# A two-layer encoder on one core: in every fourth weight step, the low part of the weights by an accumulating DMA

## The chip, the core and the metric

The kernel runs on one core of a Trainium2 chip. The metric is the device time of one execution in microseconds (us), the median of the runs; lower is better. The engines are called as the profile calls them: PE (TensorE, matrix products), PEld (its weight loads), DVE (VectorE), ACT (ScalarE), POOL (GpSimd) and SP (SyncE, which here only issues DMAs). SPq stands for SP's instruction queue. All loads of weights and inputs are issued by SP.

## What is computed

x has 256 tokens of 2048 columns, all in float32. Two layers follow each other; each one normalizes, projects, mixes, projects back, normalizes and adds:

```python
h = rmsnorm(x, norm_pre[0])                       # layer 0: gated linear attention
q, k, v, g, glr = split(h @ gla_w_in)             # 2048 x (1024 + 1024 + 2048 + 2048 + 16)
y = attention_by_chunks(q, k, v, glr) * silu(g)
x = x + rmsnorm(y @ gla_w_out, norm_post[0])      # 2048 x 2048

h = rmsnorm(x, norm_pre[1])                       # layer 1: spatial gating
u, v, g = split(h @ sgu_w_in, 3)                  # 2048 x 6144
y = gelu(u) * spatial(layernorm(gelu(v))) * silu(g)
x = x + rmsnorm(y @ sgu_w_out, norm_post[1])      # 2048 x 2048
```

The four big projections carry nearly all of the work. Their weights are read from memory once.

## The kernel before, in words

**Three products for one.** PE multiplies in float32r, which keeps fewer bits than float32. So each operand is kept as two float32r parts, high and low: the high part is the rounded value, the low part what the rounding left over. A product is the sum of three: high by high, low activations by high weights, high activations by low weights (lines 178, 179, 180).

**Groups and steps.** The columns of the weights are taken in 33 groups of up to 512 columns, in this order: two groups q (steps 0 to 15), three groups k of 352, 344 and 344 columns (16 to 39; the first of them is put together from two pieces of the weights), four groups v (40 to 71), four g (72 to 103), four of layer 0's output projection (104 to 135); then layer 1's four groups vg (136 to 167), four u (168 to 199), four sg (200 to 231) and four of its output projection (232 to 263). A group is 8 steps, and a step is two K tiles of 128 rows: one load of 128 x 1024 float32 (512 KB; 344 KB in the narrow groups). Both tiles of 128 tokens (t = 0 and t = 1) use a step's weights, so a step has 2 tokens x 2 K tiles x 3 = 12 products.

**What is done for a step.** `load` (line 91) takes a tile `raw` out of a ring of RAWS = 4 and issues the load on SP (line 98). `split` (line 105) takes tiles `whi` and `wlo` out of rings of SPLITS = 6; ACT copies `raw` to `whi` with rounding (line 110), and then DVE writes `wlo` = `raw` - `whi` (line 111). In a few steps (`pool_lo`, line 134: 0, 2, 4, 6, and 1, 3 and 5 steps behind the start of layer 1, that is 137, 139, 141) POOL does the subtraction in place of DVE.

**Order.** The program is written out by hand, and every engine takes its instructions in that order. `run` (line 188) issues the products of a step for one tile of tokens (`part`), lets each live generator take a stage (`advance`: what follows a group's products, for example the activation, the norms, the transposes), and then calls `fetch` for the steps up to AHEAD = 4 beyond the current one. So behind the products of step i for t = 0 stand the load and the split of step i + 4. At the end of a group the activation of its result for t = 0 stands on ACT just ahead of the split of the next group's step 3. Because step i + 4 stands behind the products of t = 0 alone, this split can begin only when PE is in the middle of the group's last step.

**What a tile waits for.** The load of step i + 4 waits until the split of step i has been done with its `raw` tile; the ring of four makes steps 3, 7, 11, ... share one of the four. ACT's copy for step i waits for its load and for PE's last product with the `whi` of step i - 6. SP's queue is in order too, so a load that waits holds up the loads behind it.

**POOL's other work.** POOL raises the norms to the power -0.5 (line 224), prepares the products with the gains around layer 0's output (lines 605 and 640), and scales and shifts `vg` in the u groups (line 703).

Of the kernel before, what the change touches and what calls it, by code (L numbers as in the profile page):

```python
# [9 lines left out]
F32R = mybir.dt.float32r  # L10
BF16 = mybir.dt.bfloat16
AF = mybir.ActivationFunctionType
ALU = mybir.AluOpType
PSUM = bass.MemoryType.PSUM

P = 128
# [6 lines left out]
KC = 2  # L23
LAG = 5
# [5 lines left out]
SLOTS = 24  # L30
RAWS = 4
SPLITS = 6


@with_exitstack
def trunk(
# [18 lines left out]
    nc = tc.nc  # L55
# [9 lines left out]
    of = out[0]  # L65
# [6 lines left out]
    wraw = ctx.enter_context(tc.tile_pool(name="wraw", bufs=RAWS))  # L72
    wsp = ctx.enter_context(tc.tile_pool(name="wsp", bufs=SPLITS))
    gains = ctx.enter_context(tc.tile_pool(name="gains", bufs=3))
# [12 lines left out]
    def w512(name, dtype=F32):  # L87
        return work.tile([P, 512], dtype, name=name, tag="w512")

# [1 line left out]
    def load(parts, c, fine):  # L91
        w = sum(n for _, _, n in parts)
        raw = wraw.tile([P, KC, w], F32, name="raw", tag="raw")
        at = 0
        for src, c0, n in parts:
            rows = src[c * KC * P : (c + 1) * KC * P, c0 : c0 + n].rearrange("(a p) n -> p a n", p=P)
            for ks in pieces(fine):
                nc.sync.dma_start(raw[:, ks, at : at + n], rows[:, ks, :])
            at += n
        return raw  # L100

    def pieces(fine):
        return [slice(k, k + 1) for k in range(KC)] if fine else [slice(0, KC)]

    def split(raw, eng, fine):
        shape = [P, KC, raw.shape[2]]
        hi = wsp.tile(shape, F32R, name="whi", tag="whi")
        lo = wsp.tile(shape, F32R, name="wlo", tag="wlo")
        for ks in pieces(fine):
            nc.scalar.copy(hi[:, ks], raw[:, ks])  # L110
            eng.tensor_tensor(lo[:, ks], raw[:, ks], hi[:, ks].bitcast(F32), op=ALU.subtract)  # L111
        return hi, lo

    NS = KT // KC

    class Stream:
        """Projections, column group by column group, in steps of KC K tiles; both tiles of
        tokens use a step's weights. What follows a group's products is a generator, whose
        stages come one by one between the parts that follow; a stage may ask for more parts
        before the next. Around a boundary (a group whose operand is the end of all groups  # L120
        before it) the tiles of tokens take turns of LAG steps, so that each one's products
        cover what the other waits for."""

        def __init__(self, groups, boundaries, mid):
            self.mid = mid
# [19 lines left out]
        def fetch(self, i):  # L145
            if i < len(self.steps) and i not in self.split:
                self.load(i)
                eng = nc.gpsimd if i in self.pool_lo else nc.vector
                self.split[i] = split(self.raw[i], eng, i == 0)

        def start(self, gen):
            if gen is not None:
# [35 lines left out]
        def run(self):  # L188
            freed, at = 0, 0
            for i, t in self.order:  # L190
# [4 lines left out]
                at = max(at, i)  # L195
                for j in range(at + 1, min(at + (AHEAD if at >= NS else 2), freed + SPLITS - 1) + 1):
                    self.fetch(j)
# [1 line left out]
                self.advance()  # L199

    def split_T(dst, t, c, tp):
        """Four transposed blocks, from PSUM into the two parts of a product's operand."""
        ah, al = dst
        sl = slice(t * P, (t + 1) * P)
        nc.scalar.copy(ah[c][:, :, sl], tp)  # L205
        nc.vector.tensor_tensor(al[c][:, :, sl], tp, ah[c][:, :, sl].bitcast(F32), op=ALU.subtract)  # L206
# [7 lines left out]
    def new_T(name):  # L214
        return (
            [slot(S4, F32R, f"{name}h{c}") for c in range(4)],
            [slot(S4, F32R, f"{name}l{c}") for c in range(4)],
        )
# [18 lines left out]
        return rstd(s1, D, name)  # L237

    def bcast(vecs, cs):
        """Column groups of vectors, on every partition."""  # L240
        g = gains.tile([P, 2, 512], F32, name="gb", tag="gb")
        for i, (v, c) in enumerate(zip(vecs, cs)):
            nc.sync.dma_start(
                g[:, i, :], v[c * 512 : (c + 1) * 512].unsqueeze(0).to_broadcast([P, 512])
            )
        return g

# [1 line left out]
    xs = [const.tile([P, D], F32, name=f"x{t}", tag=f"x{t}") for t in range(NT)]  # L249
    vec = const.tile([16, P], F32, name="vec")  # L250
    nc.scalar.dma_start(vec, norm_pre[0].rearrange("(a p) -> a p", p=P))
# [6 lines left out]
    make_identity(nc, ident)  # L258
    mhalf = const.tile([P, 1], F32, name="mhalf")
    nc.gpsimd.memset(mhalf, -0.5)  # L260
    # suffix sums within a chunk: U[t', t] = 1/tau where t' > t and both lie in one chunk;
    # the last two columns give the chunks' sums
    U = const.tile([P, P + 2], F32, name="U")
    nc.gpsimd.memset(U, 0.0)
    for c in range(2):
# [8 lines left out]
    gpre0 = const.tile([P, KT], F32, name="gpre0")  # L274
    bsp = const.tile([P, GROUPS], F32, name="bsp")

# [1 line left out]
    hT = new_T("hT")  # L278

    def make_hT(t, c):  # L280
        tp = transpose4(xs[t][:, c * 512 : (c + 1) * 512])
        tmp = w512("ttmp").rearrange("p (a b) -> p a b", b=P)
        gain = gpre0[:, c * 4 : c * 4 + 4].unsqueeze(2).to_broadcast([P, 4, P])
        nc.vector.tensor_tensor(tmp, tp, gain, op=ALU.mult)
        split_T(hT, t, c, tmp)
# [3 lines left out]
    groups = []  # L289

    q, k, la, ek, kd, k2, qT = ([None] * 2 for _ in range(7))
# [14 lines left out]
    for i in range(2):  # L306
        groups.append(dict(parts=[(W, q0 + i * 512, 512)], lhs=lambda: hT, done=q_done(i)))

    # the gate's weights and bias, each part at its own partitions, against the parts of the
    # low-rank activations: one pass gives all four products  # L310
    wg = [None]

    def pre_gate():
# [179 lines left out]
    for i, (c0, n) in enumerate(kcols):  # L493
        parts = [(W, k0 + c0, n)] + ([(W, l0, RANK)] if i == 0 else [])
        groups.append(dict(parts=parts, lhs=lambda: hT, done=k_done(i)))

    on = [None] * HEADS
# [30 lines left out]
    def pre_gain(key, vecs, cs):  # L528
        def f():
            st[key] = bcast(vecs, cs)  # L530
        return f
# [13 lines left out]
    def g_done(h):  # L545
        def f(t, ps):
            if t == 0:
                new_T4("ogT", h, "ogT")
            sg = w512("sg")
            nc.scalar.activation(sg, ps, AF.Silu, scale=r0[t])  # L550
            nc.vector.tensor_tensor(sg, on[h][:, t, :], sg, op=ALU.mult)
            yield 4
            split_T(st["ogT"], t, h, transpose4(sg))
        return f
# [1 line left out]
    for h in range(HEADS):  # L556
        groups.append(dict(parts=[(W, g0 + h * DV, DV)], lhs=lambda: hT, done=g_done(h)))

# [1 line left out]
    def out_groups(key, w_out, gain, name, end, extra=None):  # L560
        yg = [None] * 4
        ss = [small(f"{name}ss{t}", 4) for t in range(NT)]

        def done(c):
            def f(t, ps):
                if t == 0:
                    yg[c] = slot([P, NT, 512], F32, f"{name}g{c}")
                sumsq(ps, ss[t][:, c : c + 1])

                def scale():  # L570
                    if extra is not None:
                        extra(t, c, ps)
                    nc.vector.tensor_tensor(yg[c][:, t, :], ps, st[name][:, c % 2, :], op=ALU.mult)

                if c < 3:
                    scale()
                else:
                    s1 = small(f"{name}s{t}")
                    nc.vector.reduce_sum(s1, ss[t], axis=mybir.AxisListType.X)
                    yield from end(t, yg, rstd(s1, D, f"{name}r{t}"), scale)  # L580
            return f

        gs = [dict(parts=[(w_out, c * 512, 512)], lhs=lambda: st[key], done=done(c)) for c in range(4)]
        for c in (0, 2):
            gs[c]["pre"] = pre_gain(name, [gain] * 2, [c, c + 1])
        return gs
# [6 lines left out]

    r1 = [None] * NT

    # the second layer's operand is x1 * gain = x * gain + rstd * (y * post gain * gain)
    yp, xp = [None] * 4, [None] * 4

    def extra0(t, c, ps):
# [45 lines left out]
    groups += gs  # L645
    layer1 = len(groups)

# [1 line left out]
    W2 = sgu_w_in[0]  # L649
    vg = [None] * 4  # L650
    bst = [small(f"bst{t}", 4 * 6).rearrange("p (c s) -> p c s", s=6) for t in range(NT)]
# [42 lines left out]
    def u_done(c):  # L694
        def f(t, ps):
            if t == 0:
                u[c] = slot([P, NT, 512], F32, f"u{c}")
            nc.scalar.activation(u[c][:, t, :], ps, AF.Gelu_apprx_tanh, scale=r1[t])
            a = vg[c][:, t, :]
            mu, rv = st["ln", t]  # L700
            nc.vector.tensor_scalar(a, a, mu, rv, op0=ALU.subtract, op1=ALU.mult)  # L701
            for i, op in enumerate((ALU.mult, ALU.add)):
                nc.gpsimd.tensor_tensor(a, a, st["lng"][:, i, :], op=op)  # L703
        return f

    for c in range(4):
        groups.append(
            dict(
                parts=[(W2, c * 512, 512)], lhs=lambda: st["h2"], done=u_done(c),
# [48 lines left out]

    groups += out_groups("tT", sgu_w_out[0], norm_post[1], "y1", end1)

# [1 line left out]
    mid = {(0, 0): lambda: make_hT(1, 0), (1, 0): lambda: make_hT(0, 1)}  # L762
    for c in range(1, 4):
        mid[2 * c - 1, 1] = lambda c=c: make_hT(1, c)
# [2 lines left out]
    s = Stream(groups, [layer1, len(groups)], mid)  # L767
# [50 lines left out]
```

## Time and profile before

| | us |
|---|---|
| median of 2 runs | 775.23 |
| lowest and highest | 775.1, 775.36 |
| profiled execution: span from its first to its last instruction | 772.0 |
| PE busy in it | 755.7 |
| DVE busy | 452.9 |
| ACT busy | 353.7 |
| POOL busy | 87.6 |

The span is that of one profiled execution; 3.2 us lie between it and the median of the runs, ahead of the first and behind the last instruction. The page has the whole execution in sums and in 40 slices; the trace has every instruction with its start and duration, and says what ended the idle time ahead of it. The share of the DMA engines is a mean over the 16 that the core has.

### The profile page before, as it was taken

Reading aid. Unit: us, or ns where it says so; the run is one execution under the profiler, and the core shown is the slowest. Engines: PE = TensorE matmul, PEld = TensorE weight load, DVE = VectorE, ACT = ScalarE, POOL = GpSimd, SP = SyncE. Lnnn points to the kernel's source line nnn. Section 1 sums busy time; section 2 is a strip of 40 time slices with the busy share of each in tenths; the row PEclk is TensorE's granted clock in tenths of the full one; section 3 lists DMA queues with packets and bytes.
Section 4 is the critical chain, followed back from the end, with each engine's and each line's share of the span. In section 5 each row is a group of like instructions: output and inputs, shape, how many; then the busy total and the mean of one; then the engine's idle time right before and its main releaser. Section 6 shows DMA issues by size and latency. Waiting matters only on the chain.

```text
span 772.0 us, 9465 instructions
## 1 busy us (share of the span) xinstructions
PE 755.7 (98%) x3560; PEld 633.4 (82%) x3560; DVE 452.9 (59%) x521; ACT 353.7 (46%) x473; POOL 87.6 (11%) x81
## 2 busy tenths in 40 slices
PE   8999999999999999999989999999999999999995
PEld 6889998888888888888867888888888888888884
DVE  4666764645465545766588564555556565565443
ACT  4654753534354434444446454444335445344430
POOL 3210010000000001403041000132232000000000
PEclk9999999999999999999999999999999999999998
DMA  9576583465755567664724855666766455656633
GB/s 302 162 209 186 159 259 110 136 218 165 216 166 168 169 196 232 215 219 167 264 88 137 272 190 192 196 208 215 227 217 203 152 166 169 195 182 234 203 104 110
DMA packets 81318, 146.28 MB, mean 189 GB/s; under 512 B 7196, under 2 KB 14900, under 8 KB 81272
## 3 DMA queue, kind: packets, MB, share of 16 engines
q1 hardware_dynamic: 81240, 145.66, 59.5%
q8 instruction: 28, 0.46, 0.2%
q14 instruction: 18, 0.15, 0.1%
q10 hardware_dynamic: 32, 0.01, 0.0%
HBM read 143.55 MB, written 2.10 MB: 189 GB/s over the span
## 4 chain that ended last, share of the span: by engine, by line
PE 94%; DVE 2%; issue 1%; DMA 1%; ACT 0%; SPq 0%; POOLq 0%; POOL 0%; DVEq 0%; ACTq 0%
PE acc L180 30%; PE acc L178 30%; PE acc L179 30%; PE tp L211 2%; PE op L519 1%; DVE hp L614 1%; DMA raw<-in_gla_w_in_dram 1%; PE sc L440 1%; PE sp L371 0%; PE sc L433 0%; DVE h2l L206 0%; DVE wlo L111 0%; DVE x L752 0%; DVE x L590 0%; PE sc L446 0%
## 5 line engine op out<-in xcount | busy, mean ns | idle before, releaser
L111 DVE TENSOR_TENSOR wlo<-raw,whi 128x1024 fp32r<-128x1024 f32 (+2 forms) x257 | 316.6, 1254 | 119.6 <-ACT whi L110 119.2
L110 ACT CAST whi<-raw 128x1024 fp32r<-128x1024 f32 (+3 forms) x265 | 264.7, 1021 | 141.7 <-PE acc L179 57.5
L178 PE MATMUL acc<-whi,hTh 128*128 128x512 f32 (+2 forms) x416 | 158.7, 382 | 1.4 <-ACT hTh L205 1.4
L179 PE MATMUL acc<-whi,hTl 128*128 128x512 f32 (+2 forms) x416 | 155.9, 375 | 0.2 <-DVE hTl L206 0.2
L180 PE MATMUL acc<-wlo,hTh 128*128 128x512 f32 (+2 forms) x416 | 156.0, 375 | 0.0
L178 PE MATMUL acc<-whi,h2h 128*128 128x512 f32 x384 | 151.5, 394 | 0.0
L179 PE MATMUL acc<-whi,h2l 128*128 128x512 f32 x384 | 150.0, 391 | 0.0
L180 PE MATMUL acc<-wlo,h2h 128*128 128x512 f32 x384 | 149.8, 390 | 0.0
L178 PEld LDWEIGHTS acc<-whi,hTh 128*128 128x128 f32 x416 | 78.5, 189 | 13.3 <-ACT hTh L205 1.7
L180 PEld LDWEIGHTS acc<-wlo,hTh 128*128 128x128 f32 x416 | 78.4, 189 | 12.9
L179 PEld LDWEIGHTS acc<-whi,hTl 128*128 128x128 f32 x416 | 78.6, 189 | 12.7 <-DVE hTl L206 0.6
L180 PEld LDWEIGHTS acc<-wlo,h2h 128*128 128x128 f32 x384 | 72.4, 188 | 15.3
L178 PEld LDWEIGHTS acc<-whi,h2h 128*128 128x128 f32 x384 | 72.4, 189 | 14.4
L179 PEld LDWEIGHTS acc<-whi,h2l 128*128 128x128 f32 x384 | 72.4, 189 | 14.3
L178 PE MATMUL acc<-whi,ogTh 128*128 128x512 f32 x128 | 50.2, 392 | 0.0
L178 PE MATMUL acc<-whi,tTh 128*128 128x512 f32 x128 | 50.0, 391 | 0.0
L179 PE MATMUL acc<-whi,tTl 128*128 128x512 f32 x128 | 49.8, 389 | 0.0
L180 PE MATMUL acc<-wlo,ogTh 128*128 128x512 f32 x128 | 49.8, 389 | 0.0
L180 PE MATMUL acc<-wlo,tTh 128*128 128x512 f32 x128 | 49.8, 389 | 0.0
L179 PE MATMUL acc<-whi,ogTl 128*128 128x512 f32 x128 | 49.8, 389 | 0.0
L703 POOL TENSOR_TENSOR vg<-vg,gb 128x512 f32<-128x512 f32 x16 | 27.8, 1735 | 61.4 <-DVE vg L701 41.1
L229 ACT ACTIVATE sq<-acc 128x512 bf16<-128x512 f32 x16 | 9.5, 596 | 50.3 <-PE acc L180 50.3
(155 smaller groups left out, 586.9 us busy)
## 6 DMA issues: line engine op xcount, KB each, us to landing
raw<-in_sgu_w_in_dram SPq DMA_DIRECT2D x96, 512.0 KB, 4.8
raw<-in_gla_w_in_dram SPq DMA_DIRECT2D x79, 512.0 KB, 4.6
raw<-in_gla_w_out_dram SPq DMA_DIRECT2D x32, 512.0 KB, 5.7
raw<-in_sgu_w_out_dram SPq DMA_DIRECT2D x32, 512.0 KB, 4.8
raw<-in_gla_w_in_dram SPq DMA_DIRECT2D x16, 344.0 KB, 3.7
raw<-in_gla_w_in_dram SPq DMA_DIRECT2D x8, 336.0 KB, 3.6
x<-in_x_dram SPq DMA_DIRECT2D x8, 256.0 KB, 7.4
gb<-in_norm_post_dram SPq DMA_DIRECT2D x8, 256.0 KB, 6.2
```

What stands on the lines that cost most here:

```text
L110: nc.scalar.copy(hi[:, ks], raw[:, ks])
L111: eng.tensor_tensor(lo[:, ks], raw[:, ks], hi[:, ks].bitcast(F32), op=ALU.subtract)
L178: nc.tensor.matmul(pt, xh, wh[:, k, :], start=kt == 0, stop=False)
L179: nc.tensor.matmul(pt, xl, wh[:, k, :], start=False, stop=False)
L180: nc.tensor.matmul(pt, xh, wl[:, k, :], start=False, stop=kt == KT - 1)
L211: nc.tensor.transpose(tp[:, k, :], src[:, k * P : (k + 1) * P], ident)
L229: nc.scalar.activation(sq[:, : src.shape[1]], src, AF.Square, accum_out=dst)
L440: nc.tensor.matmul(sc[:, o + C : o + P], k2[c][:, i, o : o + P], qT[c][:, i, o + C : o + P], start=jl == 0, stop=jl == JH - 1,)
L519: nc.tensor.matmul(op, a, b, start=i == 0, stop=i == len(ops) - 1)
L614: nc.vector.scalar_tensor_tensor(hp[c], yp[c][:, t, :], r, xp[c][:, t, :], op0=ALU.mult, op1=ALU.add)
L703: nc.gpsimd.tensor_tensor(a, a, st["lng"][:, i, :], op=op)
```

## The change

A function `added` is new. It makes `wlo` = -`raw` on ACT (rounded, as `whi` is), then `whi` = `raw` on ACT, and then issues two DMAs on POOL's queue, one for each K tile of the step, that add `raw` onto `wlo` (SBUF to SBUF). `fetch` calls it, in place of `split`, for the steps 3, 7, 11, ... (every fourth) from step 8 on, where the group's weights are one piece. These are 62 of the 264 steps: 66 are every fourth, less the two in the first group and the two in the first k group. Of the 62, step 139 had its subtraction on POOL, the other 61 on DVE. The other lines of the diff take out comments.

```diff
+ADDED = 4
...
+    def added(raw):
+
+        shape = [P, KC, raw.shape[2]]
+        hi = wsp.tile(shape, F32R, name="whi", tag="whi")
+        lo = wsp.tile(shape, F32R, name="wlo", tag="wlo")
+        nc.scalar.activation(lo, raw, AF.Copy, scale=-1.0)
+        nc.scalar.copy(hi, raw)
+        for k in range(KC):
+            nc.gpsimd.dma_start(lo[:, k, :], raw[:, k, :], accum_op=ALU.add)
+        return hi, lo
...
         def fetch(self, i):
             if i < len(self.steps) and i not in self.split:
                 self.load(i)
-                eng = nc.gpsimd if i in self.pool_lo else nc.vector
-                self.split[i] = split(self.raw[i], eng, i == 0)
+                parts = self.groups[self.steps[i][0]]["parts"]
+                if len(parts) == 1 and i % ADDED == ADDED - 1 and i >= NS:
+                    self.split[i] = added(self.raw[i])
+                else:
+                    eng = nc.gpsimd if i in self.pool_lo else nc.vector
+                    self.split[i] = split(self.raw[i], eng, i == 0)
```

## Rows read from the trace of the kernel before

**Rows 1.** The page: busy time of each engine, and PE and DMA in 40 slices
```profile
PE 755.7 (98%) x3560; PEld 633.4 (82%) x3560; DVE 452.9 (59%) x521; ACT 353.7 (46%) x473; POOL 87.6 (11%) x81
...
PE   8999999999999999999989999999999999999995
...
DMA  9576583465755567664724855666766455656633
```

**Rows 2.** Waits of PE in the whole span (us in total, times, longest)
```profile
PE tp L211 <- DVE hp L614: 4.7, 3, 2.6
PE acc L178 <- ACT hTh L205: 1.4, 1, 1.4
```

**Rows 3.** Timeline of PE, two products in a row (start us, duration us, instruction)
```profile
301.00 0.39 PE L178 MATMUL acc<-whi,hTh 128*128 128x512 f32 x1
301.23 0.39 PE L179 MATMUL acc<-whi,hTl 128*128 128x512 f32 x1
```

**Rows 4.** Groups of instructions: count, busy us, mean ns, idle before with its releasers
```profile
L111 DVE TENSOR_TENSOR wlo<-raw,whi 128x1024 fp32r<-128x1024 f32 (+2 forms) x257 | 316.6, 1254 | 119.6 <-ACT whi L110 119.2
L110 ACT CAST whi<-raw 128x1024 fp32r<-128x1024 f32 (+3 forms) x265 | 264.7, 1021 | 141.7 <-PE acc L179 57.5 <-DMA raw<-in_gla_w_out_dram 19.9 <-DMA raw<-in_sgu_w_in_dram 18.2
...
L111 POOL TENSOR_TENSOR wlo<-raw,whi 128x1024 fp32r<-128x1024 f32 (+1 forms) x8 | 18.8, 2356 | 16.9 <-ACT whi L110 16.9
```

**Rows 5.** Waits of SP's queue (us in total, times, longest)
```profile
SPq L98 <- DVE wlo L111: 506.2, 229, 7.4
```

**Rows 6.** Timeline of ACT at two ends of u groups
```profile
513.24 0.69 ACT L698 ACTIVATE u<-acc,r 128x512 f32<-128x512 f32 x1 [5.97 <-PE acc L180]
513.83 1.04 ACT L110 CAST whi<-raw 128x1024 fp32r<-128x1024 f32 x1
...
535.00 0.69 ACT L698 ACTIVATE u<-acc,r 128x512 f32<-128x512 f32 x1 [5.97 <-PE acc L180]
```

**Rows 7.** Timeline of PE, the next group's step 3
```profile
522.56 0.39 PE L178 MATMUL acc<-whi,h2h 128*128 128x512 f32 x1
...
523.01 0.39 PE L180 MATMUL acc<-wlo,h2h 128*128 128x512 f32 x1
```

**Rows 8.** Line 98 from 425 to 755 us: all its loads are 512 KB
```profile
DMA to landing us min/median/max: 3.6/4.9/8.0
```

**Rows 9.** DMA queues (packets, MB, share of 16 engines) and issues (count, KB each, landing)
```profile
q1 hardware_dynamic: 81240, 145.66, 59.5%
...
gb<-in_norm_post_dram SPq DMA_DIRECT2D x8, 256.0 KB, 6.2
...
out_dram<-x SPq DMA_DIRECT2D x6, 256.0 KB, 2.5
```

**Rows 10.** ACT's activations of v, by line: ns min/median/max, first and last start
```profile
L506 ACT ACTIVATE vh<-acc,r x8: 686/688/690, 141.3 to 214.2; 128x512 fp32r<-128x512 f32 x8
```

**Rows 11.** The same for g (line 550)
```profile
L550 ACT ACTIVATE sg<-acc,r x8: 690/691/692, 236.5 to 306.1; 128x512 f32<-128x512 f32 x8
```

**Rows 12.** The same for sg, in layer 1 (line 719)
```profile
L719 ACT ACTIVATE sg<-acc,r x8: 689/690/694, 600.3 to 674.9; 128x512 f32<-128x512 f32 x8
```

**Rows 13.** Timeline of ACT in the second q group
```profile
37.89 2.93 ACT L110 CAST whi<-raw 128x1024 fp32r<-128x1024 f32 x3
```

**Rows 14.** Timeline of PE, step 11's first product with wlo
```profile
43.89 0.39 PE L180 MATMUL acc<-wlo,hTh 128*128 128x512 f32 x1
```

**Rows 15.** Timeline of DVE at the start of layer 1
```profile
393.43 3.40 DVE L111 TENSOR_TENSOR wlo<-raw,whi 128x1024 fp32r<-128x1024 f32 x1
```

**Rows 16.** Timeline of POOL in the same place
```profile
393.27 2.47 POOL L111 TENSOR_TENSOR wlo<-raw,whi 128x1024 fp32r<-128x1024 f32 x1 [0.31 <-ACT whi L110]
```

**Rows 17.** Windows: us, busy of PE, PEld, DVE, ACT, POOL, clock, DMA share, GB/s
```profile
390.00:415.00 25.00, 20.34 (x98) 15.99 (x97) 24.34 (x27) 10.69 (x18) 10.55 (x6) 0.93 0.32 105
425.00:755.00 330.00, 330.00 (x1498) 273.79 (x1497) 184.74 (x187) 146.99 (x173) 31.69 (x20) 1.00 0.60 194
755.00:772.00 17.00, 8.63 (x39) 6.80 (x37) 7.56 (x16) 1.38 (x4) 1.09 (x2) 0.84 0.36 124
```

## Prediction

> **What bounds the kernel now.** I read the page first. PE is busy for 755.7 of 772.0 us, in all but the first and last slices at 90% or more; DVE has 59%, ACT 46%, the DMA engines 50 to 70% in most slices [rows 1]. The table of PE's waits then says how little there is to win: the program's waits sum to some 6 us [rows 2]. By windows, PE is never idle from 425 to 755 us; its idle time lies in the tail, which ends in norms and stores, and in 390 to 415 us, where layer 1 starts (4.7 us) [rows 17]. Two products start 0.227 us apart [rows 3], so a step of 12 takes 2.72 us and four steps 10.9 us. DVE's 1.25 us and ACT's 1.02 us per step [rows 4] lie beside that. So taking work off DVE is worth nothing by itself except at 390 to 415 us; what decides is whether the new way of making `wlo` is in time.
>
> Two clocks tell that. The first is the ring of `raw`: SP waits 229 times, 506 us in all, for DVE's `wlo` to free a `raw` tile [rows 5]. Every fourth step owns one of the four tiles, so the added steps all share one, and its round (load, ACT, DMAs, next load) must fit into four steps of PE. The second is the lead at group ends: in the u groups ACT idles until the group's first result (513.24), then makes `whi` of the next group's step 3 (513.83 to 514.87) [rows 6]; PE takes that step's first `wlo` product at 523.01 [rows 7], 8.1 us later. Step 3 is an added step in every group.
>
> **The change part by part.** *Removed:* 61 subtractions on DVE (61 x 1.25 = 76 us) and one on POOL (2.4) [rows 4]. DVE goes from 452.9 to about 377 us. PE hides nearly all of it: gain 0. The exception is step 139: its subtraction on POOL (393.27 to 395.74) [rows 16] runs beside one on DVE that takes 3.40 us [rows 15] where the mean is 1.25 [rows 4]. Without it DVE would be free 2.2 us sooner, ahead of work that PE waits for [rows 2]. Bounds 0 and 4.7 (all of PE's idle time there [rows 17]); I take -2.
>
> *Added on ACT:* 62 copies of 1.02 us [rows 4], 63 us, ACT to 417 us of 772. They are hidden by ACT's idle time, but `-raw` stands ahead of `whi`, so `whi` comes 1 us later; with leads of 7 us that costs nothing.
>
> *Added on POOL and the DMA engines:* 124 issues, each waiting for ACT's `wlo`. Behind a waiting issue on POOL stand the powers of line 224 and lines 605, 640, 703; they stand behind the same split on ACT or DVE anyway, and POOL has 11% of work, so I take 0 for them. The trace has no DMA issued by POOL and none that adds, so D, the time from the end of ACT's `wlo` to the landing of both DMAs, is bounded by neighbours. Low: two plain 256 KB stores, 2.5 us to landing [rows 9], the second half a us behind: 3.0. High: the slowest load, 8.0 us [rows 8], and behind it one more transfer (1.65): 9.7. The 1.65 us is the engine time of 512 KB: 59.5% of 772 us for 145.66 MB [rows 9]. I take that an adding DMA reads both its source and its target, so 256 KB is worth a 512 KB load: the first lands like the median load, 4.9 us [rows 8], the second 1.65 us behind. D = 6.55 us, nearest to the loads because it shares the engines with them.
>
> The Trainium skill weighs it from both sides. "DMA: Bandwidth & Descriptors", section "Anatomy of one DMA — SWDGE (gpsimd) path", gives a fixed 2.0 us plus the bytes at 436 GB/s: 2.6 us for 256 KB, and by it D would be near 3.5 and the change free; the row of the stores (2.5 us) agrees, for transfers that hardly share the engines. "Collectives: The Full Stack", section "The bandwidth ceiling: the fold count and why AG ≠ RS ≠ AR", says that a DMA that adds runs at half the rate of a copy because it reads two sources; no run here shows it yet, and by it the doubling above stands.
>
> *The ring's round.* A load that is first behind a blocked queue should land near the shortest, 3.6 us, rather than the median 4.9 [rows 8]; I take 4.0. Then ACT 1.05 [rows 6], D 6.55, two handoffs 0.1: 11.7 us. The allowance is four steps with what PE does between them: v 11.9 us ((214.2 - 141.3 - 1.4)/6; 1.4 is the half step between the tokens) [rows 10]; g 11.4 [rows 11]; sg 12.2 [rows 12]; both output projections, vg and u 10.9 (513.24 to 535.00 is 21.8 for a group [rows 6]). So v and sg cover it. In g each of 8 rounds is 0.3 us late, in the other four stages each of 32 is 0.8 late: 2.4 + 25.6 = 28 us. The lead of 8.1 us less D leaves 1.6 us to use up before PE waits, three times (before g, at layer 1's start, behind sg): -5.
>
> *Start and narrow groups.* Step 11's `wlo` would leave ACT at 39.85 (the second of three copies from 37.89) [rows 13]; its product starts at 43.89 [rows 14]. That is 4.0 us, so PE waits 2.5 us; step 15 and the narrow groups may add a little. I take +3 (bounds 0 and 10).
>
> *Sum:* 28 - 5 + 3 - 2 = +24 us on the execution of 772.0, so a span of 796; with the 3.2 us around it, 799.
>
> **The rivals.** *The round fits.* Place: the shared `raw` tile. If D is under 5.75 us, the round is under 10.9 us and no stage is late; what is left is -2 at layer 1 and up to 2 at the start: 775 us. Up to D = 6.3 (a round of 11.45) the sum stays within 2%. For it: the DMA engines have 40% idle [rows 17] and a lone 256 KB takes 2.5 us [rows 9]. Against it: both DMAs move while three loads queue behind the freed one, and the 256 KB broadcasts in mid-stream take 6.2 us [rows 9]. This is the way in which it isn't slower. The Trainium skill's "Anatomy of one DMA", named above, is the rule by which it would come out so.
>
> *The DMAs come one behind the other.* If POOL's second issue starts late, or an adding transfer costs the engines twice what I take, D is 8.2 (one more 1.65), the round 13.35. Then every stage is late: 8 x (1.45 + 1.95 + 4 x 2.45 + 1.15) = 115, less 5, plus 8 at the start and in the narrow groups, less 2: +116, 891 us. For it: nothing in the trace tells how long POOL needs to issue. Against it: the 40% of idle engines.
>
> *DVE's relief counts for more.* The round fits and layer 1's start loses all of its 4.7 us of waiting: 771 us. More than that isn't there for the taking [rows 17], so a gain of 2% (15.5 us) can't come.
>
> **How the numbers follow.** Forecast (rounds late in five stages, D from 6.05 to 7.45) 0.42; fits (D below that) 0.34; one behind the other 0.14; relief 0.10. The forecast's own range: at a round of 12.6 us it is 8 x (0.7 + 1.2 + 4 x 1.7 + 0.4) = 73, less 5, plus 5, less 2: 846; at 11.2 us 10 - 5 + 3 - 2: 781. The whole range goes from the relief, 771, to a little over the heavy rival, 900. Two per cent is about what a measurement of this kernel can tell from no change. Slower by over 2%: 0.39 of the forecast's 0.42 and the heavy 0.14, 0.53. The rest, 0.34 + 0.10 + 0.03 of the forecast's low end, is 0.47; 0.01 of it goes to faster, for a gain that I don't see, and 0.46 to within 2%.
>
> **What would show it.** Right: PE's waits list `wlo` of the added steps behind a DMA on POOL's queue, some 20 to 30 us in all, most of it in the output projections, vg and u, little in v and sg; SP's waits name a DMA for every fourth load; the added DMAs land 4 to 6 us after issue. DVE's busy time near 377 us and ACT's near 417 show that the change does what it says. Wrong: no such waits (D too big, or loads landing faster than 4.0), or waits of 2 us and more at every fourth step (D too small), or waits behind POOL's other work, which I took for 0.

## The result, and the profile after

The changed kernel takes 803.17 us (median of 2 runs, 802.71 to 803.63) where the kernel before took 775.23: 1.0361 times the time, with a 95% interval of 1.0331 to 1.0391. The forecast was 799. The span of the profiled execution went from 772.0 to 800.9 us.

The page after: busy time of the engines, PE and DMA in 40 slices, and the two DMA queues that carry the data (packets, MB, share of 16 engines).

```profile
PE 768.5 (96%) x3560; PEld 633.9 (79%) x3560; DVE 385.6 (48%) x460; ACT 410.6 (51%) x535; POOL 186.2 (23%) x204
...
PE   8979999999999999999889999999999999999994
...
DMA  9587677588787889788775898898888877877774
...
q1 hardware_dynamic: 81240, 145.66, 55.8%
q0 software_dynamic: 17856, 31.83, 23.0%
```

Beside [rows 1], DVE has lost 67 us and ACT gained 57, POOL has 99 us more, and PE's instructions are the same in number. The DMA engines, busy for about 60% before, are now at 79%. A new queue, q0, holds the 124 DMAs that POOL issues. Its 31.83 MB cost 23.0% of 800.9 us, 5.8 us a MB; the loads of q1 cost 55.8%, 3.1 us a MB. So a byte that is added costs the engines 1.9 times what a byte loaded costs. (The Trainium skill's "Collectives: The Full Stack", in the section named in the prediction, says half the rate of a copy, for the DMAs of a collective: the 1.9 here is near that, though it is against loads from memory; no plain copy from SBUF to SBUF runs in this case.)

The new lines among the groups of the page: DVE's subtraction (line 123 now), POOL's DMAs, ACT's new copy.

```profile
L123 DVE TENSOR_TENSOR wlo<-raw,whi 128x1024 fp32r<-128x1024 f32 (+2 forms) x196 | 246.9, 1283 | 200.5 <-ACT whi L122 184.1
...
L114 POOL DMA_DIRECT2D wlo<-raw x124 | 109.3, 1034 | 497.4 <-ACT wlo L111 483.7
...
L111 ACT ACTIVATE wlo<-raw 128x1024 fp32r<-128x1024 f32 (+1 forms) x62 | 64.5, 1040 | 127.4 <-DMA raw<-in_sgu_w_in_dram 57.8
```

196 subtractions where [rows 4] have 257, and 62 copies more: the change does what it says. Now PE's waits (us in total, times, longest), and SP's.

```profile
PE acc L196 <- DMA wlo<-raw: 15.8, 15, 2.6
PE tp L227 <- DVE kd L418: 1.8, 1, 1.8
...
PE tp L227 <- DVE hp L630: 1.2, 2, 0.8
```

```profile
SPq L99 <- DMA wlo<-raw: 365.5, 58, 10.8
SPq L99 <- DVE wlo L123: 152.0, 76, 7.2
```

In [rows 2] no product waited for `wlo`; now the longest list is the low products (line 196) that wait for an adding DMA. The sum of 15.8 us isn't all: where PE's weight loads wait first, the time stands under PEld. SP, which in [rows 5] waited for DVE's `wlo` 229 times, now does so 76 times and waits for these DMAs 58 times: once for nearly each of the 62 added steps.

Two added steps in a u group, 183 and 187 (timeline, start and duration): the load, ACT's copies, POOL's two issues, PE's products with `wlo`, and the loads that waited for the landing.

```profile
542.92 0.38 SPq L99 DMA_DIRECT2D raw<-in_sgu_w_in_dram  x1
...
547.18 1.06 ACT L111 ACTIVATE wlo<-raw 128x1024 fp32r<-128x1024 f32 x1 [5.79 <-DMA raw<-in_sgu_w_in_dram]
548.15 1.03 ACT L112 CAST whi<-raw 128x1024 fp32r<-128x1024 f32 x1
...
548.54 1.76 POOL L114 DMA_DIRECT2D wlo<-raw  x2 [8.54 <-ACT wlo L111]
...
551.42 0.37 SPq L99 DMA_DIRECT2D raw<-in_sgu_w_in_dram  x1
...
554.63 0.50 PE L196 MATMUL acc<-wlo,h2h 128*128 128x512 f32 x1 [0.33 <-DMA wlo<-raw]
...
554.65 0.37 SPq L99 DMA_DIRECT2D raw<-in_sgu_w_in_dram  x1
...
556.01 1.06 ACT L111 ACTIVATE wlo<-raw 128x1024 fp32r<-128x1024 f32 x1 [0.15 <-DMA raw<-in_sgu_w_in_dram]
...
557.36 1.77 POOL L114 DMA_DIRECT2D wlo<-raw  x2 [0.27 <-ACT wlo L111]
...
566.75 0.50 PE L196 MATMUL acc<-wlo,h2h 128*128 128x512 f32 x1 [1.62 <-DMA wlo<-raw]
...
568.11 0.38 SPq L99 DMA_DIRECT2D raw<-in_sgu_w_in_dram  x1
```

The load at 542.92 is step 183's. The forecast's parts can be read off: 4.3 from the load's issue to ACT (forecast 4.0 and a handoff), 1.06 for `wlo`, 6.4 from there to the next load into this tile at 554.65 (D, forecast 6.55): a round of 11.7 us. PE takes up the second product of `wlo` in the moment in which the tile is free.

But the load at 554.65 is step 188's. Step 187's went out at 551.42, 3.2 us before step 183's DMAs had landed, behind a subtraction of DVE: it has another tile (ACT takes it up at 556.01, too soon for a load that began at 554.65). Its DMAs land last, at 568.0 (D = 10.9), and let step 191's load go at 568.11. So the added steps don't all share one tile, as the part on the kernel before and the prediction have it. In the kernel before, no load goes out before the split of the step four earlier is done. In the changed kernel the tile of an added step goes to the step four later in 36 of 61 cases and to the step five later in 25 (worked out from the semaphores that the loads wait for). What holds is that the landing stops SP's queue twice in a group: from the load at 542.92 to the one at 568.11, which are eight steps, it took 25.2 us where a group of PE has 21.8.

Time from issue to landing (least, median, greatest), first of the adding DMAs, then of the 512 KB loads from 445 to 780 us:

```profile
DMA to landing us min/median/max: 2.9/4.6/10.0
```

```profile
DMA to landing us min/median/max: 3.9/5.5/8.9
```

The first issue mostly starts 0.3 us behind ACT's `wlo`, the second 0.55 to 0.6 behind the first, and the second DMA lands 1.3 us behind the first in the median. D, worked out for the 62 steps from the end of ACT's `wlo` and the later of the two landings, has a median of 6.0 us and goes from 4.2 to 10.9.

Where the 29 us of the span went: the table has, for a stretch of steps, how much later than in the kernel before it ends (worked out from the start of each stretch's first product in the two traces; the last line is the rest of the span). The columns of the experiments below belong to the same table.

```
steps, what            after  e2   e3   e4   e5   e6   e7   e8   e9   e10
0-7     first q        -0.7 -0.7 -0.7 -0.4  1.5 -0.7 -0.4 -0.7 -0.7  1.5
8-15    second q        7.1  7.0  2.5  5.7  9.9  7.4  0.4  6.4 11.0  2.0
16-71   k, v            3.7  1.3  0.0  0.0  0.9 10.8  2.3  2.5  1.7  0.1
72-103  g               0.0  0.0  0.0  0.0  0.1 10.1  0.0  0.0  0.6  0.0
104-130 output proj. 0  8.2  5.3  1.6  3.8  4.8 13.6  8.6  3.9  7.9  1.5
131-143 layer 1 starts  1.3  7.7 -2.7  0.7 -1.0  4.3  1.3 -0.6  1.5  3.5
144-167 vg              0.0  0.7  0.0  0.0  0.6 11.5  0.0  0.0  1.2  0.0
168-199 u               5.1  9.6  0.0  0.0  4.7 14.8  4.6  5.2  1.3  0.0
200-231 sg              0.4  0.0  0.0  1.1  0.0  6.7  0.0  2.0  0.0  0.0
232-258 output proj. 1  0.8  5.2  0.0  0.0  2.0  7.0  0.0  2.3  5.1  0.0
259-end                 3.1  0.3  0.2  0.3  2.1  0.8 -0.2 -0.1  0.2 -0.1
```

By the starts of PE's products (worked out, as an estimate), 19 of the 29 us lie just ahead of products with an added step's `wlo`. Three smaller parts are of another kind. The first is PE's clock. Behind some of these waits the granted clock falls to half (the lower of its two levels, 1.2 and 2.4 GHz): from 59.6 to 66.4 us, 387.2 to 390.6, 407.7 to 411.1 and 568.1 to 571.5. Two products in the last of these, and this stretch as a window (us, busy of PE, PEld, DVE, ACT, POOL, clock, DMA share, GB/s):

```profile
568.95 0.63 PE L195 MATMUL acc<-whi,h2l 128*128 128x512 f32 x1
569.38 0.63 PE L196 MATMUL acc<-wlo,h2h 128*128 128x512 f32 x1
...
568.10:571.50 3.40, 3.40 (x8) 2.64 (x9) 0.00 (x0) 0.00 (x0) 0.00 (x0) 0.51 0.61 183
```

They start 0.43 us apart, where [rows 3] have 0.23. Each of the four stretches begins in a wait of PE for an adding DMA or within half a us of its end; the kernel before has one such stretch behind step 8, at layer 1's start (397.8 to 401.2), and e3 below, where nobody waits for the DMAs, none before its tail. The slower products cost some 7 us in place of 1 (an estimate from their distances): about 6 of the 29.

The second part is the order of POOL's queue. Its clearing of `wgr` (the tile of the gate's weights, which step 15 doesn't use) stands behind the issues of step 11, which wait for ACT; SP's loads of `wgr` wait for the clearing, and the loads of steps 14 and 15 stand behind these. POOL and SP, in the kernel before and then in the changed one:

```profile
38.95 0.95 POOL L315 MEMSET wgr<- 128x1024 f32 x1
39.93 0.34 SPq L317 DMA_DIRECT2D wgr<-in_gla_w_gate_dram  x1
```

```profile
41.39 1.63 POOL L331 MEMSET wgr<- 128x1024 f32 x1
43.05 0.34 SPq L333 DMA_DIRECT2D wgr<-in_gla_w_gate_dram  x1
```

So step 15's load goes out at 46.7 us in place of 43.3, and PE waits 1.7 and 1.4 us for its `wlo`. (e3 below has the same late load without any landing to wait for, and loses 2.5 us in this stretch.) The third part is small: in `k, v`, PE's transposes wait 1.8 us for `kd`, which stands on DVE behind a split that comes late after step 43's late load; the rest of the 3.7 us there is mostly the clock behind step 15, and no product of k or v waits for an adding DMA.

### The profile page after: what moved, and what is told of

It reads as the page before. It is cut to its first block, busy times and chain, and to the rows that moved or that the text cites. A ratio compares the mean times of both kernels' runs of the same rounds, so it can differ in the third digit from the quotient of the medians.

```text
span 800.9 us, 9809 instructions
## 1 busy us (share of the span) xinstructions
PE 768.5 (96%) x3560; PEld 633.9 (79%) x3560; DVE 385.6 (48%) x460; ACT 410.6 (51%) x535; POOL 186.2 (23%) x204
## 3 DMA queue, kind: packets, MB, share of 16 engines
q1 hardware_dynamic: 81240, 145.66, 55.8%
q0 software_dynamic: 17856, 31.83, 23.0%
## 4 chain that ended last, share of the span: by engine, by line
PE 68%; DMA 16%; DVE 6%; ACT 5%; issue 3%; POOL 1%; SPq 1%; ACTq 0%; POOLq 0%; DVEq 0%
PE acc L196 21%; PE acc L194 21%; PE acc L195 21%; DMA wlo<-raw 9%; DVE wlo L123 3%; DMA raw<-in_gla_w_out_dram 3%; ACT wlo L111 2%; DMA raw<-in_gla_w_in_dram 2%; DMA raw<-in_sgu_w_out_dram 1%; PE tp L227 1%; ACT whi L122 1%; DMA raw<-in_sgu_w_in_dram 1%; PE op L535 1%; POOL wlo L114 1%; DVE hp L630 1%
## 5 line engine op out<-in xcount | busy, mean ns | idle before, releaser
L123 DVE TENSOR_TENSOR wlo<-raw,whi 128x1024 fp32r<-128x1024 f32 (+2 forms) x196 | 246.9, 1283 | 200.5 <-ACT whi L122 184.1
L122 ACT CAST whi<-raw 128x1024 fp32r<-128x1024 f32 (+3 forms) x203 | 202.1, 1017 | 70.4 <-DMA raw<-in_gla_w_in_dram 19.7
L114 POOL DMA_DIRECT2D wlo<-raw x124 | 109.3, 1034 | 497.4 <-ACT wlo L111 483.7
L111 ACT ACTIVATE wlo<-raw 128x1024 fp32r<-128x1024 f32 (+1 forms) x62 | 64.5, 1040 | 127.4 <-DMA raw<-in_sgu_w_in_dram 57.8
L112 ACT CAST whi<-raw 128x1024 fp32r<-128x1024 f32 (+1 forms) x62 | 63.0, 1017 | 0.0
L196 PE MATMUL acc<-wlo,ogTh 128*128 128x512 f32 x128 | 51.9, 406 | 7.1 <-DMA wlo<-raw 6.5
```

The source lines that it names most:

```text
L111: nc.scalar.activation(lo, raw, AF.Copy, scale=-1.0)
L112: nc.scalar.copy(hi, raw)
L114: nc.gpsimd.dma_start(lo[:, k, :], raw[:, k, :], accum_op=ALU.add)
L196: nc.tensor.matmul(pt, xh, wl[:, k, :], start=False, stop=kt == KT - 1)
```

## The experiments

The theory was that of the prediction: the round of the shared `raw` tile is longer than four steps of PE, in some stages. The first rival: 32 MB of adding DMAs slow the loads, whoever waits for them. A later one: not the tile's round, but the lead of step 3 decides. All kernels but the last are edits of the changed one; ratios are to the kernel before on the same chip, which took 773.3 to 773.7 us there.

**Five `whi` and `wlo` tiles (e1), and five `raw` tiles with them (e2).** A fifth `raw` tile needs the room of a sixth split tile, so e1 gives that up alone.

```diff
-SPLITS = 6
+SPLITS = 5
```
```diff
-RAWS = 4
+RAWS = 5
```

> The changed kernel with five tiles each of whi and wlo in place of six; it makes room for the next kernel and is its measure. My theory (the round of the one raw tile that all added steps share takes longer than four steps of PE) and the rival (the 124 DMAs slow the weight loads by their share of the DMA engines) both say about the time of the changed kernel, 800 to 808 us: the split that decides begins at the group's end, and the sixth tile isn't what it waits for.

> The kernel of e1_splits5 with five raw tiles in place of four, so that the added steps take the tiles in turn and a round has five steps of time. By my theory the waits in the first output projection (8 us) and in the u groups (5 us) go, the loads at the start and the end come sooner too: 780 to 788 us. By the rival the engines carry the same bytes, and it stays at 798 to 808 us.

Measured: e1 818.08 us (1.0562, 1.0525 to 1.06), e2 807.99 (1.0432, 1.0355 to 1.0509). e1 missed what both theories gave; e2 missed mine and lies at the upper end of the rival's. e1 is 15 us above the changed kernel. The sixth split tile isn't the only difference: the `raw` tiles are handed out otherwise too (to the step four later in 55 of 61 cases), and these runs don't separate the two. Of the 15, 7 us lie at layer 1's start, where `fetch` is limited by the split tiles (`freed + SPLITS - 1`), and 5 in the u groups. The fifth `raw` tile (which goes to the step five later in 55 of 60 cases) gave back 10 us where 15 to 23 were to be won. The landing of e2's adding DMAs fits that:

```profile
DMA to landing us min/median/max: 2.8/6.8/10.7
```

The median is 6.8 where it was 4.6. Between issue and landing of such a DMA the loads now move 164 GB/s in the mean, where they moved 118 (worked out from q1's packets): with more loads let go, the DMAs share the engines with more of them. That this is what took back the ring's gain is argued.

**The same DMAs with nobody waiting (e3).** DVE subtracts as before; POOL issues 124 DMAs of the same size from `whi` onto two spare tiles (five split tiles, to make room).

```diff
-        nc.scalar.activation(lo, raw, AF.Copy, scale=-1.0)
         nc.scalar.copy(hi, raw)
+        nc.vector.tensor_tensor(lo, raw, hi.bitcast(F32), op=ALU.subtract)
         for k in range(KC):
-            nc.gpsimd.dma_start(lo[:, k, :], raw[:, k, :], accum_op=ALU.add)
+            nc.gpsimd.dma_start(dump[k][:, : raw.shape[2]], hi[:, k, :].bitcast(F32), accum_op=ALU.add)
```

> The subtraction is back on VectorE, ScalarE makes whi alone, and the same 124 accumulating DMAs of the same size run beside it from whi onto two spare tiles that nobody reads, so that no raw tile waits for them (five whi and wlo tiles to make room). By my theory the time goes back to 774 to 780 us. By the rival (the engines' load) it stays near 800 us, and the loads land later than before.

Measured: 775.45 us (1.0026, 1.0014 to 1.0037). The first lines of its page's queues and of PE's waits:

```profile
q1 hardware_dynamic: 81240, 145.66, 58.7%
q0 software_dynamic: 17856, 31.83, 25.0%
```

```profile
PE tp L231 <- DVE hp L634: 3.2, 4, 1.3
...
PE acc L200 <- DVE wlo L127: 2.0, 3, 1.2
```

The same MB at 84% of the engines, and PE loses nothing in k, v, g, vg, u, sg and the second output projection. The rival falls: 32 MB beside the loads cost PE nothing there as long as it doesn't wait for them, though the loads do land later, as the rival said (a median of 5.2 us over all loads, 4.7 in the kernel before). The even total hides two parts: 4.1 us lost in the second q group and the first output projection, and 2.7 won at layer 1's start, where step 139's subtraction is on DVE (see e12). In the second q group POOL's issues hold up the clearing of `wgr` as in the changed kernel (step 15's load goes out at 47.1 us); no landing is waited for.

**Every fifth step (e4), every third (e6).** 50 and 83 added steps in place of 62, on changing `raw` tiles.

```diff
-ADDED = 4
+ADDED = 5
```

> Every fifth step in place of every fourth (50 steps in place of 62), which moves the added steps over all four raw tiles. By my theory no stage has a late round any more and only the start's loss is left: 778 to 786 us. By the rival the loss goes with the number of DMAs: 28 us x 50/62 = 23, 798 us.

> Every third step (83 steps in place of 62), spread over all four raw tiles. By the theory of the round and the lead: more bytes, but a tile's next step is an ordinary one; two thirds of the added steps aren't step 3 or 7: 783 to 797 us. By a loss that goes with the number of DMAs: 28 us x 83/62 = 37, 811 us.

Measured: e4 782.58 us (1.0104, 1.0027 to 1.0181), as the theory had it: the losses in u, v and at the end are gone, though four fifths of the DMAs are there; left are the start and half of the first output projection. e6 863.31 us (1.1166, 1.1065 to 1.1267): missed by both, by 52 us and more. PE's waits in e4 and e6, and the landings in e6:

```profile
PE acc L196 <- DMA wlo<-raw: 8.5, 10, 1.9
```

```profile
PE acc L196 <- DMA wlo<-raw: 55.0, 67, 5.5
```

```profile
DMA to landing us min/median/max: 3.0/6.7/10.1
```

My expectation for e6 left out two things that its trace shows. SP's queue is blocked until one added step's DMAs have landed, and then lets three loads go at once; with every third step the next but one added step's load is the last of the three. It lands late (8.7 us in step 158's case) and its DMAs, beside the next loads, take 6.7 us each in the median. From 479.8 to 498.1 us, two such loads, six steps take 18.3 us where PE needs 16.3. With every fifth the load is the second of its burst and has five steps. So the round decides, but its length depends on the place in the burst and on the company of the DMAs, not on the tile alone.

**Steps 1 and 5 in place of 3 and 7 (e5), and the same with five `raw` tiles (e8).**

```diff
-                if len(parts) == 1 and i % ADDED == ADDED - 1 and i >= NS:
+                if len(parts) == 1 and i % ADDED == 1 and i >= NS:
```

> The same number of added steps, still one raw tile, but steps 1 and 5 of a group (9, 13, 25, ...) in place of 3 and 7. The round of the tile stays what it is (11.7 us at D of 6). What changes is the lead: the split of step 3 begins only in the middle of the group before's last step, that of steps 1 and 5 isn't tied to the group's end. Theory A (late rounds use up a lead, and PE waits only when it is gone; step 3 has 8.1 us of it, steps 1 and 5 some 12): the first output projection and the u groups absorb most of their 8 and 5 us, the start's loss stays: 780 to 792 us. Theory B (the round alone decides): 799 to 806 us.

> The kernel of e2_raws5 (808 us) with the added steps at 1 and 5 of a group. In e2_raws5 the DMAs took 8 to 12 us to land, since four loads are on their way beside them, and step 3's lead of 8 us was too short for that. If so, the same DMAs cost nothing in the u groups and the second output projection where the lead is longer: 782 to 793 us. If the ring or the engines were the cause: 802 to 812 us.

Measured: e5 798.77 us (1.0331, 1.03 to 1.0363), e8 795.70 (1.0292, 1.026 to 1.0324). e5 misses theory A and just misses B: the u groups lose 4.7 us with the long lead as with the short one, the first output projection 4.8 in place of 8.2, and the start loses more (11.4 for its two groups in place of 6.4), since POOL's clearing of `wgr` now stands behind the issues of step 13 (49.0 us) and step 15's load goes out at 54.8. A longer lead uses up the lateness of a few rounds only. e8 lies between its two cases as well (the 8 to 12 us that its expectation names are D in e2's u groups; a single DMA landed there in at most 10.7): better than e2 by 12 us, most of it at layer 1's start and in the u groups, but 5 us in u stay. There PE still waits for landings: D is 8.4 to 13.5 us in the u groups, and at steps 181, 189 and 197 POOL's scaling of `vg` stands ahead of the issue, which starts 2.0 to 3.2 us behind ACT's `wlo`. Which of these parts makes the 5 us these runs don't separate.

**Without the added steps at the start and the end (e7).**

```diff
-                if len(parts) == 1 and i % ADDED == ADDED - 1 and i >= NS:
+                if len(parts) == 1 and i % ADDED == ADDED - 1 and 2 * NS <= i < 32 * NS:
```

> The changed kernel without its added steps 11, 15 (the second q group) and 259, 263 (the end): 58 in place of 62. The trace shows 7 us lost in the second q group and 3 us behind step 259. If these are losses of those steps alone: 791 to 795 us. If the start's loss only comes later in another place: 798 to 803 us.

Measured: 791.71 us (1.024, 1.0196 to 1.0285), as expected: by the ratios to the kernel before (1.0361 and 1.024) some 9 us less for four steps of 62. 6.7 us of the start's 7.1 and all of the end's 3.1 belong to steps 11, 15, 259 and 263.

**The tile freed early (e9), the DMAs short (e10).** In e9 the DMAs read `whi` in place of `raw`; in e10 they move 64 columns of 512. Both leave out low parts of weights, as the expectations say.

```diff
-            nc.gpsimd.dma_start(lo[:, k, :], raw[:, k, :], accum_op=ALU.add)
+            nc.gpsimd.dma_start(lo[:, k, :], hi[:, k, :].bitcast(F32), accum_op=ALU.add)
```
```diff
-            nc.gpsimd.dma_start(lo[:, k, :], raw[:, k, :], accum_op=ALU.add)
+            nc.gpsimd.dma_start(lo[:, k, 0:64], raw[:, k, 0:64], accum_op=ALU.add)
```

> The added steps' DMAs read whi in place of raw, so that raw is free when ScalarE has made both copies, while PE still waits for the same two DMAs of the same size (they begin about 1 us later, with whi). It leaves out the low part of the weights of the added steps: minus whi plus whi is 0. If the round of the raw tile makes the loss, the first output projection (8 us) and the u groups (5 us) lose at most 2 us each; of the start's loss (7 us) at least the part of step 11 stays: 777 to 789 us. If it is the landing itself that comes too late for PE: 798 to 808 us.

> The same 124 DMAs with 64 columns each in place of 512 (32 KB in place of 256 KB), still onto wlo and out of raw. It leaves out the low part of the other columns of the added steps. It measures what of the 6 us from ScalarE's wlo to the landing of both is fixed: I expect 3 to 4 us fixed, so a round of some 9 us, under the 10.9 us of four steps, and 774 to 782 us. If the fixed part were nearly all of it, 795 us or more.

Measured: e9 801.98 us (1.0369, 1.0341 to 1.0398), e10 781.17 (1.01, 1.0079 to 1.0122). In e9 SP no longer waits for the DMAs (first fence), yet PE does, and longer than in the changed kernel (second), since their landing has gone up again (third):

```profile
SPq L99 <- DVE wlo L123: 359.0, 174, 7.5
SPq L99 <- ACT whi L112: 147.0, 44, 6.8
```

```profile
PE acc L196 <- DMA wlo<-whi: 21.2, 19, 4.3
```

```profile
DMA to landing us min/median/max: 3.3/6.7/10.7
```

The u groups behave as the round has it (1.3 us in place of 5.1); the first output projection doesn't (7.9), the second loses 5.1 that it hadn't lost, and the start 11. Part of that is e9's own: its DMAs begin 1 us later. So my theory in its strict form, that the held tile makes the loss, falls. What stands is a pair of limits on one thing, the landing of the DMAs: while the tile holds SP's queue back, few loads run beside the DMAs and they land in 4.6 us, but the loads come late; when the queue runs free, the loads come in time and the DMAs land in 6.7. Either way some `wlo` is late. e10 shows the other end: its DMAs land in 3.0 us,

```profile
DMA to landing us min/median/max: 2.1/3.0/6.0
```

D is 3.8 us in the median, a round some 9 (added up as in the prediction), and v, g, vg, u, sg and the second output projection lose nothing with SP's queue still blocked 59 times. Here the tile does go to the step four later, in 60 of 61 cases: the ring of the prediction, with a short landing, fits. Of D's 6.0 us, so, 3.8 are left with an eighth of the bytes.

**Step 139 alone: by DMAs (e11), and by DVE (e12).** e12 is the kernel before with `POOL = (1, 5)`.

```diff
-                if len(parts) == 1 and i % ADDED == ADDED - 1 and i >= NS:
+                if i == 139:
```
```diff
-POOL = (1, 3, 5)
+POOL = (1, 5)
```

> One added step alone, step 139, whose subtraction was on GpSimd just where layer 1 begins. The prediction took -2 us for it (VectorE's subtraction beside it took 3.40 us in place of 1.25). If so: 771 to 774 us beside 773.3 for the kernel before on that chip, that is 0.995 to 0.999 of it. If the landing of its DMAs is late there: 1.000 to 1.004.

> The kernel before with one edit: step 139's subtraction on VectorE in place of GpSimd, no DMA at all. In e3_aside, where it was so, layer 1's start was 2.7 us shorter. If that is the whole of it: 0.996 to 0.998 of the kernel before, the fastest of all here. If VectorE, busy for 24 of 25 us there, has no room for it: 1.000 or more.

Measured: e11 771.09 us (0.9966, 0.9955 to 0.9977), e12 771.59 (0.9976, 0.9967 to 0.9986). Both beat the kernel before, and the two can't be told apart. DVE's subtraction of step 138 in e11, and in e12:

```profile
393.68 1.21 DVE L123 TENSOR_TENSOR wlo<-raw,whi 128x1024 fp32r<-128x1024 f32 x1
```

```profile
394.15 1.21 DVE L111 TENSOR_TENSOR wlo<-raw,whi 128x1024 fp32r<-128x1024 f32 x1
```

1.21 us where [rows 15] have 3.40 beside POOL's subtraction [rows 16]. PE's wait for `hp`, 4.7 us in [rows 2], is 1.8 us in e11 and 2.2 in e12. A VectorE that is busy for 24 of 25 us [rows 17] takes on 1.2 us more of work in e12 and ends sooner: POOL's subtraction beside it had cost it 2.2, and from the first norm's sum to the last one of this stretch DVE takes 26.4 us in place of 28.7.

## Why the prediction was right, and where it wasn't

*What bounds the kernel; the work taken off DVE.* Right. DVE's 67 us brought nothing by themselves; the time went where PE waits for the new `wlo`, 19 of the 29 us directly.

*ACT's copies and POOL's issues.* ACT's are as forecast (64.5 us against 63). DVE fell to 386 us, not 377: its other subtractions got a little slower (1283 ns in place of 1254). What stands behind a waiting issue on POOL was taken for 0, and that failed at the start: the clearing of `wgr`, which the prediction doesn't name, came 2.4 us later behind step 11's issues and held back SP's loads by 3.5. Elsewhere POOL's own work holds up few issues: in the u stage the longest gap between ACT's `wlo` and POOL's issue is 1 us (step 171).

*D.* Forecast 6.55, median 6.0. Its working held: an added byte costs the engines 1.9 loaded ones (2 was assumed), and the second DMA lands 1.3 us behind the first (1.65 was taken). The formula of the Trainium skill's "DMA: Bandwidth & Descriptors", in the section named in the prediction (2.6 us for 256 KB), gives too little here: none of the DMAs of 256 KB in the changed kernel landed in under 3.2 us (the 2.9 above is one of 172 KB), and their median is 4.6.

*The round.* Forecast 11.7 us, and step 183's tile has 11.7. But the ring for which the rounds were added up is not the one of the changed kernel. "Every fourth step owns one of the four tiles, so the added steps all share one" is how the ring of the kernel before works; in the changed one the tile of an added step goes to the step five later in 25 of 61 cases, mostly every other time, and the next added step then waits for a subtraction of DVE. So the sum of eight equal rounds a stage isn't what happened, and that it came near the loss in two stages is luck. That the landing stops SP's queue, and that PE then waits for `wlo`, is as forecast.

*The steps that failed.* The sum, +24, is near the measured +29 partly by luck, because errors cancel. Beside the ring itself:

- One D was taken for all stages: "in the other four stages each of 32 is 0.8 late". In vg and the second output projection D was mostly 5.2 to 6.3, and they lost 0.8 us together where the term had 6.4 each. In the first output projection and in u, where the broadcasts of gains move beside the DMAs, single D's went up to 8.9 and 10.9, and the two lost 13 us, which is what the term had for them (3 of it by the clock).
- The lead was taken as 1.6 us. Behind sg it was 5.4 (step 235's first DMA lands that much ahead of its product); the second output projection used it up, and it was 0.2 at step 251.
- The start was sized +3 and lost 7.1 in its second group: by step 11's landing, by step 15's load, which is 3.5 us late behind POOL's queue and which the prediction mentions as "may add a little", and by the clock.
- The end was left out: step 263's `wlo` is late as well, and behind it no stage comes that could catch up (3.1 us; e7 takes it away).
- "-2" at layer 1's start came out as +1.3: the relief is real (e11, e12: -1.7 and -2.3 in that stretch), but the DMAs of steps 135 and 139 land too late there.
- The sum has no term for the clock behind PE's waits, about 6 us net.

The allowances by stage were right for v, g and sg: by them only sg loses anything, 0.4 us.

*The rivals.* "The round fits" is what happens in v, g, vg and nearly in sg, and in e4's v, g, vg, u and second projection. "One behind the other" didn't happen: POOL issues the second 0.55 us behind the first.

## What to carry to other kernels

When work moves from an engine to a DMA, ask when its result lands and what waits for it: here a 1.25 us subtraction became a wait of 6 us for a landing, and the time was lost where PE and SP's queue waited for it. Freeing the source early didn't help by itself (e9); a short landing (e10) and fewer, spread steps (e4) did. The engines' share tells little: the same 32 MB cost 4 us at most when nobody waited (e3) and 29 us when PE did. Look at what stands behind a waiting issue in the issuing engine's queue. Don't take from the source which tile of a ring a step gets: read from the trace which load waits for what. And look where two engines subtract side by side: one line that moves a subtraction off POOL beside a busy VectorE was worth more (-0.24%) than any of the versions with many DMAs.

## What the hardware showed that I hadn't expected

The landing time of the adding DMAs goes with what the loads move beside them. With 110 to 123 GB/s of loads between issue and landing (e4, e1, the changed kernel, e7; worked out from q1's packets) the median is 4.4 to 5.0 us; with 138 it is 5.5 and 6.7 (e5, e6), with 149 to 168 it is 6.2 to 7.4 (e3, e9, e2, e8). It is 3.0 with an eighth of the bytes (e10, 116 GB/s). Whether SP's queue is stopped doesn't decide it by itself: in e2 SP waits 57 times for these DMAs as well. POOL starts two issues only 0.55 us apart although each is shown as some 1.0 us long. And PE's granted clock fell to half behind several waits of 1.4 to 2.6 us, though not behind every one: behind the wait of 1.9 us at step 263 it stayed up until the tail.
